# Splitting the dense weights in two GpSimd loads instead of on ScalarE and VectorE

## The chip, the core and the metric

The kernel runs on one core of a Trainium2 chip. The metric is the device time of one execution in microseconds; the median of two runs is 1895.24 us (1895.2 to 1895.29). Engines are named as in the profile: PE is TensorE, with PEld its weight loads, DVE is VectorE, ACT is ScalarE, POOL is GpSimd, SP is SyncE. SPq, ACTq and POOLq are the queues that these engines' own sequencers work off, and L233 is line 233 of the kernel before.

## The reference

One inference step of a two-layer streaming encoder, for 512 prompt tokens and 32 sample tokens of width 1024, all in float32. Layer 0 mixes tokens with an S5 state-space model and a gated unit, layer 1 with retention (4 heads). Each layer then attends to 256 memory tokens and ends in a ConvFFN of width 2816. Nearly all of the arithmetic is dense products of the 544 tokens with weight matrices:

```python
def conv_ffn(h, conv_state, w_up, conv_w, conv_b, w_down):
    u = h.astype(F32) @ w_up.astype(F32)
    a, g = jnp.split(u, 2, axis=-1)
    ext = jnp.concatenate([conv_state.astype(F32), a], axis=1)
    conv = cw[0] * ext[:, 0:l] + cw[1] * ext[:, 1:l + 1] + cw[2] * ext[:, 2:l + 2] + conv_b
    y = (jax.nn.gelu(conv) * g) @ w_down.astype(F32)
```

```python
for each layer:  x += mixer(rms(x));  x += memattn(rms(x), mem);  x += convffn(rms(x))
```

## The kernel before

Tokens stand along the free dimension (544 columns, taken as two halves of 272), channels on the 128 partitions. A product of float32 accuracy is made from operands in two parts: a first part, `hi`, rounded to the format float32r, in which TensorE multiplies, and a second part, `lo`, the rest. Of the four products of parts three are computed.

The weights lie in HBM as tiles: one contiguous chunk of 128 x 1024 numbers (512 KB) holds all that one output tile of 128 channels needs of 8 key tiles. `weights` (L209) brings a tile in: SP loads it into a buffer `wr`, ACT copies it with rounding into `wh` (L206), DVE subtracts and writes the rest to `wl` (L207). Each of the three names has three buffers, so a load into `wr` needs the subtraction of the tile three before to be over, and the rounding into `wh` needs TensorE to be through with the tile three before.

`dense_k` (L228) multiplies one key tile: 3 pairs of parts by 2 halves of the tokens, 6 matmuls. `dense` (L236) does that for all key tiles of an output tile, 48 matmuls for 8 of them. There are 240 such weight tiles outside the first stage: 8 of the S5's gated unit (`w_glu`), 16 each of the memory attention's queries and outputs (`w_q`, `w_o`), 44 each of the ConvFFN's two up projections (`w_a`, `w_g`), 48 of its down projection (`w_d`; 32 of them hold 7 key tiles), 48 of the retention's projections (`w_r`) and 16 of its output (`w_ro`).

The first stage (`phase1`) computes the S5 layer and, in its gaps, the memory's keys and values; layer 1's part of these goes through `weights` too. Then come the gated unit, attention of layer 0, ConvFFN of layer 0, retention, attention of layer 1, ConvFFN of layer 1 and the last norm. The attention also calls `weights` with buffers of its own (`into`) for the memory's keys and values.

In the ConvFFN (`ffn`, L1064 on) 8, 7 and 7 pairs of tiles of `w_a` and `w_g` are followed by 8 tiles of `w_d`. For each pair POOL has five small instructions: a memset (L1083) and a copy (L1084) into the convolution's input, two copies of its last columns to an output (L1088, L1089), and the product for the 32 sample tokens (L1096).

The order of each engine's instructions is made by the framework's scheduler, which simulates the program with costs of its own when the kernel is built. Each engine then works through its list in order; an instruction that waits holds up all behind it on that engine.

Of the kernel before, what the change touches and what calls it, by code (L numbers as in the profile page):

```python
# [9 lines left out]
F32 = mybir.dt.float32  # L10
# [3 lines left out]
OP = mybir.AluOpType  # L14
# [5 lines left out]
KT = D // P            # channel tiles  # L20
TP = 512               # prompt tokens
TS = 32                # sample tokens
# [3 lines left out]
NM = 256               # memory tokens  # L26
FF = 2816
NF = FF // P
H = 4                  # heads (memory attention and retention)
EPS = 1e-6  # L30
GN_EPS = 1e-5
G = 64                 # S5 groups
C = 16                 # channels of a group
NP = 32                # pairs of groups
L = 8                  # S5 chunk
POS = 70               # dummy, 64 prompt chunks, dummy, 4 sample chunks
SLOT = 560             # elements of a general slot
# phase 1: microseconds of TensorE's work on the memory's projections between the steps of S5
F_START, F_DISC, F_NORM, F_MAT = 0.5, 28, 2, 13
KV_US = 3.5  # L40
KV_SPLIT = (1,)          # layers whose memory projections take operands in two parts
KV_RMS, KV_ROW = 1, 4      # key tiles after which the memory's norm is worked out, and applied
# steps of S5 for an eighth of the groups (M matrices, P phases, S states, C carry, O outputs, F fill)
PROLOGUE = (("M", 0), ("P", 0), ("S", 0), ("M", 1), ("C", 0), ("F", 6))
ORDER = (("S", 1), ("C", 1), ("O", 0), ("F", 4), ("M", 2), ("F", 5))
FGROUPS = (8, 7, 7)    # ConvFFN tiles between down projections
# [6 lines left out]
def constants():  # L53
    """Arrays that depend on shapes alone."""
# [27 lines left out]
def w_tiles(w, mt=None):  # L82
    """[K, M] -> [m tile, 128 of k, K/128 * 128 of m]: one contiguous chunk for an output tile."""
    k, m = w.shape
    a = w.reshape(k // P, P, m // P, P).transpose(2, 1, 0, 3)
    return a.reshape(m // P, P, (k // P) * P)


def layout(inp):
# [10 lines left out]
    def cols(a):                      # [.., n*128] -> [128, .. * n]  # L100
        a = a.reshape(-1, a.shape[-1] // P, P)
        return a.transpose(2, 0, 1).reshape(P, -1)
# [4 lines left out]
    def pair(a):                      # [G, 64] -> [(g2, p), pair]  # L107
        return a.reshape(NP, P).T

    def both(a):                      # [G, 64] -> [(2, p), G]  # L110
        return np.concatenate([a.T, a.T], axis=0)
# [7 lines left out]
    cr, ci = f["ssm_c_re"][0], f["ssm_c_im"][0]      # [G, C, 64]  # L119
# [6 lines left out]
    rt, it = cr.transpose(2, 0, 1), ci.transpose(2, 0, 1)          # [64, G, C]  # L126
    ca = np.stack([np.concatenate([rt, it]), np.concatenate([it, rt])])   # [2, 128, G, C]
    d["ca"] = ca.reshape(2, P, KT, 8 * C).transpose(2, 1, 0, 3).reshape(KT, P, 256)

    def rows(a):                      # [1024] -> [(jj, c), G]  # L130
        return np.tile(a.reshape(G, C).T, (L, 1))
# [7 lines left out]
    # values: [layer, half of columns, quarter of k, 128, 2 k tiles * 512]  # L139
# [13 lines left out]
    d["w_r"] = w_tiles(wq)            # q 8, k 8, v 16, g 16 tiles  # L153
# [17 lines left out]
class Kernel:  # L171
# [7 lines left out]
    # ---- tiles  # L179
# [13 lines left out]
    def psum(self, name, two, one):  # L193
        """TensorE's accumulators of a part of the program: two banks each, and one each."""
        self.two, self.one = two, one
        return self.tc.tile_pool(name=name, bufs=1, space=PSUM)
# [7 lines left out]
    # ---- weights: loaded, and split into parts of 12 and 12 bits  # L204
# [4 lines left out]
    def weights(self, src, n=1024, into=None, pool=False):  # L209
        raw = self.main.tile([P, 1024], F32, tag="wr", bufs=3, name=self.name("wr"))  # L210
# [10 lines left out]
    def mm3(self, out, a, b, start, stop):  # L221
        """out (+)= a^T b for operands in two parts."""
# [20 lines left out]
    def dense_open(self, src, xs):  # L243
        """The first operands of an output tile."""
# [10 lines left out]
    def dense2(self, srcs, xs, late=1, hooks=()):  # L255
        """Two output tiles, the last operands of both behind all others; hooks go in between."""
# [15 lines left out]
    def parts(self, src):  # L272
        """src [P, T] -> its two parts, in general slots."""
# [4 lines left out]
    # ---- norms: operands are gain * x; 1 / rms comes in where a product leaves PSUM  # L278
# [29 lines left out]
    def rsqrt_of(self, m, r, tmp):  # L308
        """r = m^-1/2: a first guess from the exponent's bits, and three steps r <- r (1.5 - 0.5 m r^2)."""
# [13 lines left out]
    def resid_cols(self, ps):  # L323
        """1 / rms of the tokens, 128 of them in a column; ps [128, 5] of PSUM."""
# [12 lines left out]
    def along_row(self, ps, rc, blocks):  # L337
        """Columns rc laid along the free dimension of all partitions, in PSUM."""
# [3 lines left out]
    def resid_r(self):  # L342
        """Two hooks that give 1 / rms of the tokens along a row of all partitions, self.r."""
# [19 lines left out]
    # ---- program  # L363
    def run(self):
        nc, tc, io = self.nc, self.tc, self.io
        self.ones = self.cp.tile([P, P], F32, tag="ones", name="ones")
# [3 lines left out]
        with tc.tile_pool(name="s5", bufs=1) as sp, self.psum("psum0", 0, 8) as self.pp:  # L370
            self.sp = sp
            self.phase1(sp)
        self.xp = self.ctx.enter_context(tc.tile_pool(name="x", bufs=1))
# [18 lines left out]
    def final(self):  # L392
        """The last norm: turned to tokens by rows, scaled by 1 / rms where it leaves PSUM."""
# [30 lines left out]
    # ---- memory keys and values  # L424
    def kv_units(self):
        """The projections of both layers, in pieces that fill gaps: (microseconds of TensorE, emit)."""
# [22 lines left out]
        def rms():  # L449
            """1 / rms of the memory's tokens: along a row, and in columns."""  # L450
# [14 lines left out]
        def operand(l):  # L465
            """gain * memory"""
# [28 lines left out]
        def product(l, out, a, ca, b, cb, k):  # L495
            """out (+)= a[:, ca]^T b[:, cb], in one or in two parts."""
# [50 lines left out]
    # ---- S5  # L547
    def cmul(self, eng, o, a, b, t, eng2=None):
        """o = a b of complex pairs; t: two temporaries of the same shape. o may not alias a or b."""
# [9 lines left out]
    def phase1(self, sp):  # L559
# [43 lines left out]
        # inputs in the S5 layout: [(7 - token of chunk, channel), group, chunk]  # L603
# [4 lines left out]
        # discretisation, for columns of pairs (32) and of groups (64)  # L608
# [8 lines left out]
        def exp_acc(out, x, t):  # L617
            """exp to float32's accuracy: 2^k times a polynomial."""
# [33 lines left out]
        # powers 0..8 of a = rho (cos, sin)  # L652
# [18 lines left out]
        # b_bar = (a - 1) / lam * b, times the norm's gains  # L671
# [23 lines left out]
        # u = x / rms(x)  # L695
# [26 lines left out]
        # unit phases of a^8 to the power of the chunk, and its magnitude  # L722
# [7 lines left out]
        def unit(c):  # L730
            """c / |c|, for |c| near 1"""
# [43 lines left out]
        def matrices(e):  # L775
            """What a chunk's inputs give to the state at its end, and to its own outputs."""
# [5 lines left out]
            # a^lag b_bar, as [(g2, p), pair, lag, c]; the second holds minus the imaginary part  # L782
# [31 lines left out]
        def states(e):  # L814
            """Chunk inputs to the state, turned back by the chunk's phase, scanned, turned forth."""
# [46 lines left out]
        def carry(e):  # L862
            """What the state before a chunk gives to its tokens: Re(c a^(l+1) x)."""
# [72 lines left out]
    # ---- memory attention  # L936
    def attention(self, ap, l):
# [33 lines left out]
        def soft(rows, b0, b1, src, pr, st):  # L971
            """Softmax of scores / 16, whose queries still lack 1 / rms."""
# [30 lines left out]
        def turn(pr, pss):  # L1003
            """The weights, keys by rows."""
# [4 lines left out]
            # the sample's, from the cache  # L1009
# [53 lines left out]
    # ---- ConvFFN  # L1063
    def ffn(self, l):  # L1064
# [11 lines left out]
        for n, size in enumerate(FGROUPS):  # L1076
            ys = []
            for _ in range(size):
# [3 lines left out]
                # [2 zeros, prompt, 2 cached rows, sample]  # L1082
# [26 lines left out]
    # ---- retention  # L1109
    def retention(self, rp):  # L1110
# [26 lines left out]
        def rope(tile0):  # L1137
            """Two tiles of a projection, rotated: in float32, and in parts."""
# [32 lines left out]
        def scores(d, h):  # L1171
            d.decay = decay = st([P, TP], "decay")
            nc.sync.dma_start(out=decay, in_=io["decay"][h])
            # keys by token, with the decay to the end
# [14 lines left out]
            # the sample's scores  # L1189
# [4 lines left out]
            # scores with decay, [key, query]  # L1194
# [34 lines left out]
        def outputs(d, h):  # L1229
            """By token, normalised."""  # L1230
# [131 lines left out]
```

## Time and profile before

| | |
|---|---|
| runs | 1895.2 to 1895.29 us, median 1895.24 |
| profiled execution | span 1893.0 us; the median lies 2.2 us above it |
| PE busy | 1820.2 us, 96% |
| DVE busy | 1086.7 us, 57% |
| ACT busy | 611.6 us, 32% |
| POOL busy | 384.7 us, 20% |
| mean granted TensorE clock | 0.980 |
| DMA | 178.02 MB, mean 94 GB/s; SP's queue 27.4% of 16 engines |

Times are those of one execution. In a group's row, the number behind x is how many instructions it holds, then come busy us, mean ns of one, idle time of the engine just before them and what ended it. In a row of waits stand: who waited for whom, us in total, how often, the longest. Matmuls overlap, so their mean duration is longer than the distance between them.

### The profile page before, as it was taken

Reading aid. Unit: us, or ns where it says so; the run is one execution under the profiler, and the core shown is the slowest. Engines: PE = TensorE matmul, PEld = TensorE weight load, DVE = VectorE, ACT = ScalarE, POOL = GpSimd, SP = SyncE. Lnnn points to the kernel's source line nnn. Section 1 sums busy time; section 2 is a strip of 40 time slices with the busy share of each in tenths; the row PEclk is TensorE's granted clock in tenths of the full one; section 3 lists DMA queues with packets and bytes.
Section 4 is the critical chain, followed back from the end, with each engine's and each line's share of the span. In section 5 each row is a group of like instructions: output and inputs, shape, how many; then the busy total and the mean of one; then the engine's idle time right before and its main releaser. Section 6 shows DMA issues by size and latency. Waiting matters only on the chain.

```text
span 1893.0 us, 32752 instructions
## 1 busy us (share of the span) xinstructions
PE 1820.2 (96%) x13785; PEld 1730.6 (91%) x13785; DVE 1086.7 (57%) x1848; ACT 611.6 (32%) x901; POOL 384.7 (20%) x439
## 2 busy tenths in 40 slices
PE   7868899999999999999999999999999999999998
PEld 6457789999999999999899899998999999999998
DVE  9999856545544535555644646546655554453553
ACT  3132454433323323333223122223444332232333
POOL 7685611011211202121000100100101121120221
PEclk9888989999999999999999999999999999999998
DMA  6434344122222222232222222222411222222221
GB/s 214 132 114 124 120 133 144 68 86 79 90 90 88 78 92 90 72 109 82 76 85 94 79 79 73 90 79 86 138 68 56 87 84 88 90 84 95 90 71 67
DMA packets 65970, 178.02 MB, mean 94 GB/s; under 512 B 8928, under 2 KB 18528, under 8 KB 65824
## 3 DMA queue, kind: packets, MB, share of 16 engines
q1 hardware_dynamic: 65536, 175.79, 27.4%
q8 instruction: 108, 1.77, 0.4%
q14 instruction: 38, 0.31, 0.1%
q10 hardware_dynamic: 288, 0.15, 0.0%
HBM read 162.78 MB, written 10.77 MB: 92 GB/s over the span
## 4 chain that ended last, share of the span: by engine, by line
PE 83%; DVE 2%; issue 1%; ACT 1%; ACTq 0%; DVEq 0%
PE ps L233 74%; PE ps L224 2%; PE ps L225 2%; PE ps L226 2%; PE ps L1286 1%; DVE wl L207 0%; PE ps L1275 0%; PE ps L1248 0%; PE ps L1008 0%; PE ps L1222 0%; ACT wh L206 0%; PE bank L1022 0%; DVE xl L292 0%; PE ps L329 0%; PE ps L403 0%
## 5 line engine op out<-in xcount | busy, mean ns | idle before, releaser
L206 ACT CAST wh<-wr 128x1024 fp32r<-128x1024 f32 (+1 forms) x256 | 264.6, 1037 | 810.2 <-PE ps L233 626.8
L233 PE MATMUL ps<-xh,wh 128*128 128x272 f32 x2432 | 507.5, 290 | 5.4 <-DVE x L356 3.6
L233 PE MATMUL ps<-xl,wh 128*128 128x272 f32 x2432 | 503.6, 288 | 0.0
L233 PE MATMUL ps<-xh,wl 128*128 128x272 f32 x2432 | 502.3, 288 | 0.0
L233 PE MATMUL ps<-r,wh 128*128 128x272 f32 x2688 | 449.2, 289 | 3.0 <-ACT r L901 1.6
L233 PEld LDWEIGHTS ps<-xh,wh 128*128 128x128 f32 x2432 | 380.7, 188 | 11.1 <-ACT r L298 3.7
L233 PEld LDWEIGHTS ps<-r,wh 128*128 128x128 f32 x2688 | 380.2, 189 | 6.4 <-ACT r L206 3.0
L233 PEld LDWEIGHTS ps<-xh,wl 128*128 128x128 f32 x2432 | 382.0, 188 | 2.3 <-issue 2.3
L233 PEld LDWEIGHTS ps<-xl,wh 128*128 128x128 f32 x2432 | 383.0, 189 | 0.3
L207 DVE TENSOR_TENSOR wl<-wr,wh 128x1024 fp32r<-128x1024 f32 (+1 forms) x256 | 321.8, 1260 | 92.3 <-ACT wh L206 84.2
L233 PE MATMUL ps<-r,wl 128*128 128x272 f32 x1344 | 278.0, 288 | 0.0
L233 PEld LDWEIGHTS ps<-r,wl 128*128 128x128 f32 x1344 | 211.2, 189 | 0.0
L356 DVE TENSOR_TENSOR x<-ps,x 128x544 f32<-128x544 f32 x96 | 69.3, 724 | 234.9 <-PE ps L233 234.7
L301 POOL TENSOR_TENSOR acc<-acc,r 128x544 f32<-128x544 f32 x36 | 58.8, 1633 | 453.1 <-ACT r L298 444.6
L1088 POOL COPY nco<-r 128x2 f32<-128x2 f32 x44 | 13.9, 315 | 374.5 <-DVE r L1086 374.5
L1095 DVE TENSOR_TENSOR r<-ps,rr 128x544 f32<-128x544 f32 x44 | 31.9, 725 | 96.7 <-PE ps L233 96.7
L1085 DVE TENSOR_TENSOR r<-ps,rr 128x272 f32<-128x272 f32 x44 | 19.4, 442 | 117.4 <-PE ps L233 117.4
L1146 POOL TENSOR_TENSOR r<-r,r 128x544 f32<-128x544 f32 x8 | 10.8, 1353 | 339.9 <-ACT wh L206 326.0
L1096 POOL TENSOR_TENSOR r<-r,r 128x32 f32<-128x32 f32 x44 | 34.3, 780 | 206.2 <-ACT wh L206 186.2
L206 ACT CAST r<-r 128x544 fp32r<-128x544 f32 x84 | 52.5, 650 | 65.8 <-POOL r L1096 26.2
L1093 DVE SCALAR_TENSOR_TENSOR r<-r,conv,r 128x546 f32<-128x546 f32 x88 | 69.1, 785 | 3.5 <-ACT r L1091 1.9
L207 DVE TENSOR_TENSOR r<-r,r 128x544 fp32r<-128x544 f32 x84 | 59.3, 729 | 14.5 <-ACT r L206 14.3
(354 smaller groups left out, 2109.0 us busy)
## 6 DMA issues: line engine op xcount, KB each, us to landing
wr<-in_w_r SPq DMA_DIRECT2D x48, 512.0 KB, 3.2
wr<-in_w_a SPq DMA_DIRECT2D x44, 512.0 KB, 3.2
wr<-in_w_g SPq DMA_DIRECT2D x44, 512.0 KB, 3.2
wr<-in_w_d SPq DMA_DIRECT2D x32, 448.0 KB, 3.2
wr<-in_w_k SPq DMA_DIRECT2D x16, 512.0 KB, 4.9
wr<-in_w_v SPq DMA_DIRECT2D x16, 512.0 KB, 3.6
wr<-in_w_q SPq DMA_DIRECT2D x16, 512.0 KB, 4.0
wr<-in_w_o SPq DMA_DIRECT2D x16, 512.0 KB, 3.3
```

What stands on the lines that cost most here:

```text
L206: self.nc.scalar.copy(hi, src)
L207: (self.nc.gpsimd if pool else self.nc.vector).tensor_tensor(out=lo, in0=src, in1=hi.bitcast(F32), op=OP.subtract)
L224: mm(out, lhsT=a[0], rhs=b[0], start=start, stop=False)
L225: mm(out, lhsT=a[0], rhs=b[1], start=False, stop=False)
L226: mm(out, lhsT=a[1], rhs=b[0], start=False, stop=stop)
L233: mm(ps[:, h, :TH], lhsT=ws[wi], rhs=x[xi][:, h * TH:(h + 1) * TH], start=start and n == 0, stop=stop and n == 2)
L301: add.tensor_tensor(out=self.acc, in0=self.acc, in1=sq, op=OP.add)
L356: self.nc.vector.tensor_tensor(out=self.halves(x), in0=src, in1=self.halves(x), op=OP.add)
L1085: V.tensor_tensor(out=ext[:, 2:2 + TH], in0=pa[:, 0, :TH], in1=r[:, :TH], op=OP.mult)
L1093: V.scalar_tensor_tensor(out=cv, in0=ext[:, t:t + W], scalar=cw[:, t, f:f + 1], in1=cv, op0=OP.mult, op1=OP.add)
L1095: V.tensor_tensor(out=self.halves(gr), in0=pg[:, :, :TH], in1=self.halves(r), op=OP.mult)
L1096: PL.tensor_tensor(out=gr[:, TP:], in0=gr[:, TP:], in1=cv[:, TP + 2:W], op=OP.mult)
```

## The change

After the first stage, `weights` no longer uses `wr`, the rounding copy and the subtraction. GpSimd issues a load from HBM straight into `wh`; since `wh` is float32r and the source float32, this transfer rounds. ScalarE then writes `wh` times -1 into `wl`. GpSimd issues a second load of the same 512 KB from HBM, which adds to what is in `wl`. So `wl` becomes the weight less its first part. In the first stage (`self.plain`), and where `weights` is given buffers, the old way stays under the name `weights_plain`. The other lines of the diff drop comments and docstrings.

```diff
     def weights(self, src, n=1024, into=None, pool=False):
+
+        if into is not None or self.plain:
+            return self.weights_plain(src, n, into, pool)
+        hi = self.main.tile([P, 1024], F32R, tag="wh", bufs=3, name=self.name("wh"))
+        lo = self.main.tile([P, 1024], F32R, tag="wl", bufs=3, name=self.name("wl"))
+        hi, lo = hi[:, :n], lo[:, :n]
+        self.nc.gpsimd.dma_start(out=hi, in_=src)
+        self.nc.scalar.activation(out=lo, in_=hi.bitcast(F32), func=AF.Copy, scale=-1.0)
+        self.nc.gpsimd.dma_start(out=lo, in_=src, accum_op=OP.add)
+        return hi, lo
+
+    def weights_plain(self, src, n=1024, into=None, pool=False):
         raw = self.main.tile([P, 1024], F32, tag="wr", bufs=3, name=self.name("wr"))
         self.nc.sync.dma_start(out=raw[:, :n], in_=src)
...
     def run(self):
         nc, tc, io = self.nc, self.tc, self.io
+        self.plain = True
...
             self.phase1(sp)
+        self.plain = False
```

In the changed kernel the three new lines are L216 (first load), L217 (negation) and L218 (accumulating load).

GpSimd's order changes most. Before, in the middle of layer 0's ConvFFN, it holds the five small instructions of each pair of tiles, one pair after the other (`r` are general buffers, `nco` the output of last columns):

```order
L1083 MEMSET r_4725 128x2
L1084 COPY r_4725<-cconv 128x2
L1088 COPY nco_4461<-r_4725 128x2
L1089 COPY nco_4461<-r_4725 128x2
L1096 TENSOR_TENSOR r_4734<-r_4734,r_4733 128x32
```

The same place on GpSimd in the changed kernel, two weight tiles of `w_a` and two of `w_g` (the small instructions are the same, 14 lines further down in the file):

```order
L216 DMA wh_4975<-in_w_a 128x1024
L1110 TENSOR_TENSOR r_4833<-r_4833,r_4832 128x32
L1097 MEMSET r_4953 128x2
L1098 COPY r_4953<-cconv 128x2
L218 DMA wl_4976<-in_w_a 128x1024
L216 DMA wh_5029<-in_w_g 128x1024
L1102 COPY nco_4435<-r_4953 128x2
L1103 COPY nco_4435<-r_4953 128x2
L218 DMA wl_5030<-in_w_g 128x1024
L216 DMA wh_5104<-in_w_a 128x1024
```

The 480 loads now stand between the small instructions. In 191 of the 240 tiles, as here, a tile's accumulating load stands directly ahead of the next tile's first load; in the other 49 the next tile's first load is ahead of it.

TensorE's order has changed at the start of many tiles. Before, in the same ConvFFN, where one tile (`wh_4804`) ends and the next (`wh_4880`) begins; `xh` and `xl` are the two parts of the tokens' operands:

```order
L233 MATMUL ps_4801<-xh_4310,wl_4805 128x272 x2
L233 MATMUL ps_4877<-xh_3914,wh_4880 128x272 x2
L233 MATMUL ps_4877<-xl_3915,wh_4880 128x272 x2
L233 MATMUL ps_4877<-xh_3914,wl_4881 128x272 x2
L233 MATMUL ps_4877<-xh_3932,wh_4880 128x272 x2
```

At such a place in the changed kernel, with `wh_4846` of `w_a` and `wh_4900` of `w_g`:

```order
L245 MATMUL ps_4770<-xh_4286,wl_4772 128x272 x2
L245 MATMUL ps_4845<-xh_3896,wh_4846 128x272 x2
L245 MATMUL ps_4845<-xl_3897,wh_4846 128x272 x2
L245 MATMUL ps_4899<-xh_3896,wh_4900 128x272 x2
L245 MATMUL ps_4899<-xl_3897,wh_4900 128x272 x2
L245 MATMUL ps_4845<-xh_3896,wl_4847 128x272 x2
L245 MATMUL ps_4845<-xh_3914,wh_4846 128x272 x2
```

The first four matmuls of the next tile, which need only its first part, are moved ahead of the matmuls that need this tile's second part.

## The prediction

> **What bounds the kernel now.** I read the page's busy shares first, then the stretches before and after 300 us, then the chain that ended last in order of time, then the waits, then the way of one weight tile through its queues.
>
> ```profile
> span 1893.0 us, 32752 instructions
> PE 1820.2 (96%) x13785; PEld 1730.6 (91%) x13785; DVE 1086.7 (57%) x1848; ACT 611.6 (32%) x901; POOL 384.7 (20%) x439
> 0.00:300.00 300.00, 244.77 (x1704) 204.29 (x1705) 260.03 (x484) 104.65 (x181) 174.05 (x169) 0.90 0.44 142
> 300.00:1893.00 1593.00, 1575.38 (x12083) 1526.35 (x12081) 826.63 (x1365) 506.91 (x721) 210.67 (x271) 1.00 0.25 85
> 600.00:700.00 100.00, 100.00 (x800) 100.00 (x799) 50.06 (x69) 29.45 (x35) 18.12 (x29) 1.00 0.26 87
> ```
>
> In the rows of stretches the numbers are PE, PEld, DVE, ACT and POOL busy, then the granted clock, the DMA share and GB/s. TensorE lies idle for 300.00 - 244.77 = 55.2 us in the first 300 us, which the change leaves nearly alone (it keeps the old loads there), and for 17.6 us in the other 1593 us, at a clock of 1.00. In the ConvFFN (600 to 700) it never stops: 800 matmuls in 100 us, 0.125 us each. A weight tile of 8 key tiles is 48 matmuls, 6.0 us; one of the down projections' smaller tiles, with 7, is 42, 5.25 us.
>
> ```profile
> 393.50 35.62 PE ps L233 x281
> 446.42 392.82 PE ps L233 x3132
> 883.09 1.06 ACT wh L206
> 884.17 1.23 DVE wl L207
> 959.96 47.99 PE ps L233 x382
> 1007.98 1.05 ACT wh L206
> 1490.23 386.98 PE ps L233 x3084
> ```
>
> These are pieces of the chain (start, length, what). Both ConvFFN layers are one unbroken run of dense matmuls (L233), 393 and 387 us. One retention head lasts 1007.98 - 883.09 = 124.9 us and ends with a run of eight tiles (382 matmuls). VectorE's subtraction appears only in between heads, 1.23 us each time.
>
> ```profile
> PE ps L233 <- DVE x L356: 3.6, 1, 3.6
> PE ps L233 <- ACT wh L206: 1.8, 2, 0.9
> ACT wh L206 <- PE ps L233: 626.8, 181, 14.2
> SPq L211 <- DVE wl L207: 1377.2, 242, 29.6
> L207 DVE TENSOR_TENSOR wl<-wr,wh 128x1024 fp32r<-128x1024 f32 (+1 forms) x256 | 321.8, 1260 | 92.3 <-ACT wh L206 84.2
> ```
>
> The dense matmuls waited for weights 1.8 us in all. The other way round, the rounding on ScalarE waited 626.8 us for TensorE to let go of a buffer, and the loads on SyncE's queue 1377.2 us for the raw buffer. So the old split is ready early everywhere; the 1.26 us subtraction lies wholly beside matmuls. Nothing that leaves VectorE can be won back except a few us at the heads' starts.
>
> **The change part by part.** *Removed:* 240 subtractions, VectorE's time beside other work, worth nothing but the 1.23 us at the start of each of four heads: -5 us. The 240 issues that leave SyncE's queue free transfers that nothing waits for: 0. *Kept in size:* ScalarE's rounding copy becomes a copy times -1 of the same tile.
>
> ```profile
> L206 ACT CAST wh<-wr 128x1024 fp32r<-128x1024 f32 x224 | 234.8, 1051 | 720.5 <-PE ps L233 561.4 <-issue 106.7 <-PE bank L226 24.8
> wr<-in_w_a SPq DMA_DIRECT2D x44, 512.0 KB, 3.2
> L211 SPq DMA_DIRECT2D wr<-in_w_a x44: 327/328/328, 405.1 to 1795.0; - x44
> DMA packets 65970, 178.02 MB, mean 94 GB/s; under 512 B 8928, under 2 KB 18528, under 8 KB 65824
> q1 hardware_dynamic: 65536, 175.79, 27.4%
> L1089 POOL COPY nco<-r 128x2 f32<-128x2 f32 x44 | 44.8, 1018 | 0.0
> L1088 POOL COPY nco<-r 128x2 f32<-128x2 f32 x44 | 13.9, 315 | 374.5 <-DVE r L1086 374.5
> L1083 POOL MEMSET r<- 128x2 f32 x44 | 4.2, 96 | 0.0
> L703 POOL TENSOR_TENSOR r<-r,r 128x560 f32<-128x560 f32 x7 | 17.2, 2452 | 0.4
> ```
>
> *Moved:* what used to be a short line (load, 1.05 us on ScalarE, 1.26 us on VectorE) with loads running three raw buffers ahead becomes load, 1.05 us on ScalarE, second transfer, and both transfers are issued by GpSimd, in order. In the program's order for GpSimd the accumulating load of a tile stands ahead of the first load of the next one in 191 of 240 cases. GpSimd therefore waits at the accumulating load until the first load has landed and ScalarE has negated it; what stands behind that wait is the next tile's first load, and behind this TensorE. The raw buffer that used to uncouple tiles is gone. So the pace is the sum of one tile's steps:
>
> 1. Issue of the accumulating load on GpSimd. SyncE's issue takes 0.328 us; GpSimd's other instructions take from 0.096 to 2.452 us. Bounds 0.33 and 2.45; I take 1.0, by the row nearest to it in kind and place, a small instruction of the ConvFFN (L1089, 1018 ns).
> 2. The accumulating transfer. A plain 0.524 MB costs 27.4% x 1893.0 x 0.524 / 175.79 = 1.55 us of all 16 DMA engines. The addition reads two operands and writes one. Bounds 1.55 (no dearer than a load) and 4.65 (each of three passages priced like a load); I take twice, 3.1. It is issued first on the queue, so I take it that the next load's packets follow it; the next load's issue on GpSimd is covered by it.
> 3. The next load's own packets: 1.55.
> 4. The rest of a landing: 3.2 from issue to landing, less 0.33 and 1.55: 1.3.
> 5. The negation: 1.05.
>
> Sum 1.0 + 3.1 + 1.55 + 1.3 + 1.05 = 8.0 us a tile. Where the next load stands ahead (49 of 240 tiles, 30 of the ConvFFN's 136) a landing and a negation, 2.35 us, run beside the other tile: 2.35 x 30/136 = 0.5 less. I take 7.5 us a tile. All bounds low: 0.33 + 1.55 + 1.55 + 1.3 + 1.05 - 0.5 = 5.3; all high: 2.45 + 4.65 + 1.55 + 1.3 + 1.05 - 0.5 = 10.5.
>
> Of TensorE's side: a ConvFFN layer is 68 tiles, 52 of 48 matmuls and 16 of 42, 3168 matmuls x 0.1255 us (392.82 / 3132) = 398 us, 5.85 a tile. GpSimd's own instructions (L1083 to L1096) stand between a load and its accumulation and lie beside the landing.
>
> - ConvFFN: 136 x (7.5 - 5.85) = +224.
> - Retention: 16 tiles a head need 16 x 7.5 = 120 us of 124.9; only the run of eight is short: three tiles are ready, five come 1.5 us late, 7.5 x 4 heads = +30.
> - The gated unit of S5 (8 tiles) and the two output projections (281 matmuls, 6 tiles each in a row): (5 + 3 + 3) x 1.5 = +17. The query projections lie between other work: 0.
> - Heads' starts: -5.
>
> Together +266 on the span's 1893.0: 2159. The median of the runs, 1895.24, lies 2.2 above the span, so 2161; I say 2160.
>
> Two rules of the Trainium skill bear on step 1 and step 4. L1088 and L1089 are the same copy and take 315 and 1018 ns, and the memset ahead of them 96: something beside them stretches GpSimd's reads. The Trainium skill (SBUF — State Buffer, Who interferes with whom) says that a VectorE instruction with two inputs in SBUF holds up GpSimd instructions that read SBUF, not those that only write. By this an issue, which writes descriptors, would be nearer to 0.33; the tile would take 6.8 us and the kernel about 2045. The trace agrees so far as copies and memset go; an issue it doesn't show. The Trainium skill (DMA: Bandwidth & Descriptors, Latency and other measured facts) puts the first byte at about 1 us for loads issued by GpSimd and about 0.6 for the others: 0.4 more in step 4, 7.9 us a tile, an estimate of about 2240. No row here has a GpSimd load, so I leave both out of the sum.
>
> **The rivals.**
>
> *Hidden after all.* If the accumulating transfer costs like a load and the issue like SyncE's, the tile takes 5.3 us against 5.85 and TensorE never waits. Then only the -5 us remain: 1890. For it: the low bounds, and three buffers leave 2 x 6.0 = 12.0 us from release to use, while the steps in a row are 1.0 + 2.9 (a landing less its issue) + 1.05 + 1.0 + 2.9 + 1.55 = 10.4. Against it: it needs both low ends, and the queue's order lets no two tiles overlap. It decides at 5.85 us a tile. This is the side of not slower.
>
> *The accumulating transfer is the bound.* If its price is at or above the upper end, or casting makes the first load dear too, a tile takes 10.5 us: ConvFFN 136 x 4.65 = 632, retention 4 x (168 - 125) = 172, the other 40 tiles some 80 (420 us against the 340 that TensorE spends there), so 2780. For it: nothing in the trace shows a transfer that computes, and this is the term with the widest bounds. Against it: the engines are at 27% now and the bytes only grow threefold or so.
>
> *Freed VectorE makes the kernel faster.* VectorE is busy 57% and loses some 300 us. But all of TensorE's idle time after 300 us is 17.6 us; even the whole of it gives 1878, under 1%.
>
> *The change does not do what it says:* were the first load not rounded, the second part would be zeros; as many instructions on as many bytes, and the same time.
>
> **How the numbers follow.** The pace of about 7.5 us (6.3 to 9) has 0.66, hidden 0.12, the transfer as the bound 0.18, faster through gaps 0.02, something else 0.02. The main case's own span: at 6.3 us a tile 136 x 0.45 = 61, and some 5 for the rest: 1960; at 9 us 428 + 76 for heads (4 x (144 - 125)) + 40: 2440. The range 1940 to 2680 takes in these and the nearer half of the dear transfer, at 10.0 us a tile 564 + 140 + 60 = +764, 2660; outside lie hidden, faster, and the far end of the third, 0.18 in all. About 2% (38 us) is what a measurement of this kernel can tell from no change. Faster 0.02, within 2% 0.12, slower 0.86.
>
> **What would show it.** Right: TensorE in the ConvFFN busy about 80% instead of 100, its waits on the accumulating load's wl, evenly at every tile; GpSimd idle before L218 for ScalarE's L217, and ScalarE before L217 for the landing; a ConvFFN layer of 510 us; retention heads lengthened by under 10 us. Wrong: waits on wh instead (the first load is the dear one); TensorE waiting nowhere (hidden); DMA engines busy above 90% (third case); an issue on GpSimd of 2 us or more (step 1), or a landing well over 3.2 us with idle engines (step 4).

## The result, and the profile after

The changed kernel takes 2170.78 us (median of 2 runs, 2166.18 to 2175.38) against 1895.24 us (1895.2 to 1895.29) before: 1.1455 times as long, 95% interval 1.1397 to 1.1512. The profiled execution has a span of 2164.3 us, 271.3 more than before.

The first page and the stretches of the changed kernel, with the columns as in the prediction (TensorE's matmuls, its weight loads, VectorE, ScalarE and GpSimd busy, granted clock, DMA share, GB/s):

```profile
span 2164.3 us, 32986 instructions
PE 1913.3 (88%) x13785; PEld 1797.0 (83%) x13785; DVE 804.3 (37%) x1608; ACT 608.0 (28%) x901; POOL 629.3 (29%) x919
q0 software_dynamic: 69120, 247.49, 50.8%
300.00:2164.30 1864.30, 1674.54 (x12150) 1599.61 (x12149) 562.29 (x1138) 507.85 (x727) 448.26 (x735) 0.96 0.60 137
600.00:700.00 100.00, 87.55 (x657) 85.61 (x657) 21.21 (x36) 21.05 (x24) 23.63 (x44) 0.97 0.62 143
600.00:900.00 300.00, 260.27 (x1918) 254.79 (x1918) 70.82 (x122) 69.78 (x82) 75.28 (x150) 0.95 0.62 140
```

TensorE does the same 13785 matmuls. It lies idle for 2164.3 - 1913.3 = 251.0 us (72.8 before), and is busy for 93.1 us more: both are new. In the ConvFFN it does 657 matmuls in 100 us where it did 800. The DMA engines are far from full on the mean, 0.62.

The waits of the changed kernel (who waits, for what, us in total, times, the longest), and then what its trace tells of the accumulating load, L218:

```profile
POOL wl L218 <- ACT wl L217: 1023.8, 216, 8.7
POOL wh L216 <- PE ps L245: 301.1, 112, 24.8
ACT wl L217 <- DMA wh<-in_w_d: 196.1, 43, 9.6
PE ps L245 <- DMA wl<-in_w_d: 44.9, 22, 3.6
```

```profile
L218 POOL DMA_DIRECT2D wl<-in_w_q x16: 854/886/916, 300.8 to 1555.2; - x16
who waited for it (us, times):
  PEld ps L245: 196.5, 107
  PE ps L245: 172.2, 98
...
DMA to landing us min/median/max: 5.0/5.5/8.9
```

Before, ScalarE waited for TensorE. Now TensorE waits for the second part (98 times in a matmul, 107 times in a weight load), GpSimd waits 1023.8 us in front of the accumulating load for the negation, and ScalarE waits for landings of the first part. In the ConvFFN this reads as follows, on GpSimd (start, length, what) and for the negation on ScalarE:

```profile
701.98 0.87 POOL L218 DMA_DIRECT2D wl<-in_w_g  x1 [6.54 <-ACT wl L217]
702.53 0.87 POOL L216 DMA_DIRECT2D wh<-in_w_a  x1
...
710.43 0.89 POOL L218 DMA_DIRECT2D wl<-in_w_a  x1 [6.59 <-ACT wl L217]
711.03 0.86 POOL L216 DMA_DIRECT2D wh<-in_w_g  x1
...
719.16 0.87 POOL L218 DMA_DIRECT2D wl<-in_w_g  x1 [6.51 <-ACT wl L217]
```

```profile
709.08 1.06 ACT L217 ACTIVATE wl<-wh 128x1024 fp32r<-128x1024 f32 x1 [4.72 <-DMA wh<-in_w_a]
```

The next first load goes 0.55 us after the accumulating one; 6.55 us later the negation starts, it takes 1.06, and 0.29 later the next accumulating load goes: 8.45 us for a tile, and 8.73 for the one after it.

Where the 271.3 us lie, by the same places in both traces (in each ConvFFN the first and the last copy of the convolution's last columns to their output, L1088 for the first and L1089 for the last before, L1102 and L1103 after; and the first rounding of the keys, kth, in the first and the last retention head):

| stretch | before, us | after, us | more |
|---|---|---|---|
| start to the first ConvFFN's first copy | 448.3 | 478.2 | 29.9 |
| first ConvFFN, first to last copy | 338.6 | 420.1 | 81.5 |
| its last tiles, to the first head | 97.4 | 116.4 | 19.0 |
| first to fourth head | 374.9 | 408.6 | 33.7 |
| to the second ConvFFN's first copy | 232.9 | 249.6 | 16.7 |
| second ConvFFN, first to last copy | 338.7 | 417.0 | 78.3 |
| to the end | 62.2 | 74.4 | 12.2 |

### The profile page after: what moved, and what is told of

Read it like the earlier page. It is cut to its first block, busy times and chain, and to the rows that moved or that the text cites. A ratio compares the mean times of both kernels' runs of the same rounds, so it can differ in the third digit from the quotient of the medians.

```text
span 2164.3 us, 32986 instructions
## 1 busy us (share of the span) xinstructions
PE 1913.3 (88%) x13785; PEld 1797.0 (83%) x13785; DVE 804.3 (37%) x1608; ACT 608.0 (28%) x901; POOL 629.3 (29%) x919
## 3 DMA queue, kind: packets, MB, share of 16 engines
q0 software_dynamic: 69120, 247.49, 50.8%
## 4 chain that ended last, share of the span: by engine, by line
issue 42%; PE 24%; POOL 12%; DMA 12%; DVE 8%; ACT 1%; POOLq 0%; DVEq 0%; ACTq 0%
PE ps L245 19%; POOL wl L218 4%; POOL wh L216 3%; DMA wl<-in_w_g 2%; DMA wh<-in_w_a 2%; DMA wl<-in_w_d 1%; DMA wh<-in_w_q 1%; DMA wl<-in_w_a 1%; POOL acc L313 1%; PE ps L236 1%; PE ps L238 1%; PE ps L237 1%; DMA wl<-in_w_ro 1%; DMA wl<-in_w_o 1%; DMA wh<-in_w_d 1%
## 5 line engine op out<-in xcount | busy, mean ns | idle before, releaser
L245 PE MATMUL ps<-xh,wl 128*128 128x272 f32 x2432 | 517.9, 296 | 89.9 <-DMA wl<-in_w_a 39.2
L217 ACT ACTIVATE wl<-wh 128x1024 fp32r<-128x1024 f32 (+1 forms) x240 | 250.7, 1044 | 966.0 <-DMA wh<-in_w_d 196.1
L245 PE MATMUL ps<-r,wh 128*128 128x272 f32 x2688 | 472.9, 301 | 5.3 <-ACT r L915 2.2
L245 PEld LDWEIGHTS ps<-r,wh 128*128 128x128 f32 x2688 | 406.3, 201 | 9.0 <-ACT r L206 3.0
L245 PEld LDWEIGHTS ps<-xh,wh 128*128 128x128 f32 x2432 | 391.8, 193 | 11.7 <-issue 8.8
L245 PE MATMUL ps<-r,wl 128*128 128x272 f32 x1344 | 295.1, 304 | 82.9 <-DMA wl<-in_w_d 44.9
L245 PEld LDWEIGHTS ps<-r,wl 128*128 128x128 f32 x1344 | 222.9, 200 | 93.2 <-DMA wl<-in_w_d 51.0
L218 POOL DMA_DIRECT2D wl<-in_w_r x48 | 42.0, 874 | 229.1 <-ACT wl L217 221.8
L218 POOL DMA_DIRECT2D wl<-in_w_d x48 | 42.3, 882 | 216.0 <-ACT wl L217 205.2
L218 POOL DMA_DIRECT2D wl<-in_w_a x44 | 39.0, 886 | 225.1 <-ACT wl L217 204.1
L218 POOL DMA_DIRECT2D wl<-in_w_g x44 | 38.5, 875 | 171.0 <-ACT wl L217 162.6
```

What stands on the lines that cost most here:

```text
L217: self.nc.scalar.activation(out=lo, in_=hi.bitcast(F32), func=AF.Copy, scale=-1.0)
L218: self.nc.gpsimd.dma_start(out=lo, in_=src, accum_op=OP.add)
L245: mm(ps[:, h, :TH], lhsT=ws[wi], rhs=x[xi][:, h * TH:(h + 1) * TH], start=start and n == 0, stop=stop and n == 2)
```

## The experiments

The theory is that GpSimd's queue sets the pace, because one tile's steps stand in a row on it, and that the accumulating transfer is the dearest of them. The rivals are the number of buffers, the transfers' price as such, and TensorE being disturbed by the accumulating writes. Each kernel was timed beside runs of the kernel before on the same chip, whose median was 1894.2 to 1894.9 us.

### One half of the change at a time

**The addition left out** (the second load overwrites the negative):

```diff
-        self.nc.gpsimd.dma_start(out=lo, in_=src, accum_op=OP.add)
+        self.nc.gpsimd.dma_start(out=lo, in_=src)
```

> The changed kernel, but the second load overwrites instead of adding: the addition is left out, wl holds the rounded weight, all waits, issues and their order stay. My theory (the pace is the sum of one tile's steps in GpSimd's order): the accumulating transfer falls from 3.1 to 1.55 us, the tile from 7.2 us (50 tiles from 600.60 to 959.55 us in the changed kernel) to 5.6, under TensorE's 5.85, so 1900 to 1960 us. Rival, too few buffers (a tile takes a third of the way from a buffer's release to the end of its next use): a third of 1.55 less, 6.7 us a tile, 2050 to 2100 us. Rival, the wait for two landings alone counts and the addition costs nothing: 2170 us.

Measured: 1933.19 us, ratio 1.0202 (1.0186 to 1.0217). This is in the theory's range. GpSimd's order and the buffers are as in the changed kernel (49 first loads stand ahead in both), only the addition is gone, and with it 238 of the 276 us. The transfer is not all that got shorter: the second load's issue on GpSimd takes 0.53 us where it took 0.88, and it lands after 3.7 us where it landed after 5.5 (medians).

**Only the accumulating load** (SyncE loads the raw tile, ScalarE rounds and negates, GpSimd adds):

```diff
-        self.nc.gpsimd.dma_start(out=hi, in_=src)
+        raw = self.main.tile([P, 1024], F32, tag="wr", bufs=3, name=self.name("wr"))[:, :n]
+        self.nc.sync.dma_start(out=raw, in_=src)
+        self.nc.scalar.copy(hi, raw)
```

> Only the second half of the change: the raw weight comes by SyncE's queue into wr and ScalarE rounds it into wh as before, then negates it, and GpSimd issues only the accumulating load. My theory: no first load stands behind GpSimd's wait any more, the way of a tile from a buffer's release is 1.05 + 1.05 + 0.87 + 5.5 = 8.5 us against 11.7 to 12, so 1890 to 1915 us. Rival, the addition's transfer is by itself too dear: the same two passages of the DMA engines are there, so it stays at 2100 us or more. Rival, too few buffers: 1900 us too, since the way is 8.5 us.

**Only the rounding load** (SyncE's raw load and VectorE's subtraction stay):

```diff
+        raw = self.main.tile([P, 1024], F32, tag="wr", bufs=3, name=self.name("wr"))[:, :n]
+        self.nc.sync.dma_start(out=raw, in_=src)
         self.nc.gpsimd.dma_start(out=hi, in_=src)
-        self.nc.scalar.activation(out=lo, in_=hi.bitcast(F32), func=AF.Copy, scale=-1.0)
-        self.nc.gpsimd.dma_start(out=lo, in_=src, accum_op=OP.add)
+        self.nc.vector.tensor_tensor(out=lo, in0=raw, in1=hi.bitcast(F32), op=OP.subtract)
```

> Only the first half of the change: GpSimd issues the rounding load into wh, SyncE a second plain load into wr, VectorE subtracts as before; no negation, no accumulating load. My theory: GpSimd waits only for buffers, so 1885 to 1900 us, and DMA traffic doubles without harm. Rival, a rounding load issued by GpSimd is itself dear or late: TensorE waits for wh, 1950 us or more.

Measured: 1936.13 us (ratio 1.0213, 1.0179 to 1.0246) and 1922.37 us (1.0139, 1.0121 to 1.0157). Both forecasts missed by some 20 us; neither half alone costs what the two cost together. By the marks of the table above, the rounding half alone loses nothing between the first and the last copy of a ConvFFN (-1.0 and -1.4 us); its loss lies in the stretches around the memory attentions (12.8 us before the first ConvFFN, 17.9 before the second). Which wait costs it there was not followed up. The accumulating half loses 4.7 and 8.1 us in the ConvFFN layers, and the rest elsewhere. GpSimd's queue in the page of the kernel with the accumulating loads alone, and of that with the rounding loads alone (packets, MB, share of 16 engines):

```profile
q0 software_dynamic: 34560, 123.75, 38.3%
```

```profile
q0 software_dynamic: 34560, 123.75, 20.1%
```

That is the price of each: 38.3% of 1934.0 us over 240 tiles is 3.09 us of all 16 engines for an accumulating load, and 20.1% of 1924.5 us is 1.61 us for a rounding one (means over all tiles, of which 32 hold 448 KB and not 512). The bytes counted are the same.

### Order and buffers

**The next tile's first load ahead of the accumulating load.** In the changed kernel it stands ahead at 49 of 240 tiles; here at 239. A list of the coming tiles gives the next source:

```diff
+        nxt = self.first()
...
+            with self.tc.issue_after(nxt[1].ins):
+                self.nc.gpsimd.dma_start(out=lo, in_=src, accum_op=OP.add)
```

> The changed kernel with GpSimd's order written out: each tile's first load is issued ahead of the accumulating load of the tile before it, at all tiles instead of 49 of 240; buffers still three. My theory: a landing and a negation now run beside the other tile; what is left is that the load ahead must wait for the release of a buffer, then 0.55 + 0.87 us of issues and 5.5 us of landing, 7.3 us to the next tile's use, and two tiles take 7.3 + 5.85, 6.6 us a tile: 2000 to 2050 us. Rival, too few buffers from the start: no gain or a loss, 2170 us or more. Rival, the DMA engines' price of the addition: 2170 us.

Measured: 2186.46 us, ratio 1.1532 (1.1493 to 1.157). The theory's forecast failed: the order alone brings nothing, and the time is in the rivals' range. The wait had moved, as the kernel's waits and its GpSimd rows show:

```profile
POOL wh L232 <- PE ps L292: 1351.1, 227, 30.0
```

```profile
704.70 0.55 POOL L232 DMA_DIRECT2D wh<-in_w_a  x1 [4.43 <-PE ps L292]
705.23 0.92 POOL L222 DMA_DIRECT2D wl<-in_w_g  x1
...
714.21 0.60 POOL L232 DMA_DIRECT2D wh<-in_w_g  x1 [7.63 <-issue]
714.81 0.92 POOL L222 DMA_DIRECT2D wl<-in_w_a  x1
...
719.22 0.55 POOL L232 DMA_DIRECT2D wh<-in_w_a  x1 [2.73 <-PE ps L292]
```

Now the first load waits for TensorE to let go of a buffer, and the accumulating load of the tile in hand stands behind that wait: two tiles take 719.22 - 704.70 = 14.52 us. The landing of an accumulating load, whose packets now follow a first load's, had a median of 7.9 us. So from the release to the landing pass 0.5 + 7.9 = 8.4 us, and with three buffers only one tile of matmuls, 5.85 us, lies beside them.

**A fourth buffer for first parts,** first alone, and then with that lookahead. Two general slots fewer make the room:

```diff
-        t = self.main.tile([P, SLOT], dt, tag="r", bufs=28, name=self.name("r"))
+        t = self.main.tile([P, SLOT], dt, tag="r", bufs=26, name=self.name("r"))
...
-        hi = self.main.tile([P, 1024], F32R, tag="wh", bufs=3, name=self.name("wh"))
+        hi = self.main.tile([P, 1024], F32R, tag="wh", bufs=4, name=self.name("wh"))
...
```

> The changed kernel with four buffers for first parts instead of three (two general slots fewer make the room); GpSimd's order of instructions is the same. Theory (queue order): load, landing, negation and accumulating load of one tile still follow one another on GpSimd's queue, some 8 us a tile whatever the number of buffers, so 2150 to 2180 us, as the changed kernel. Rival (buffers): the next load waits for TensorE to let go of a buffer, so a fourth one gives a tile's time of slack and the time falls clearly, to 2050 us or less.

> The kernel with the next tile's first load issued ahead of the accumulating load, and four buffers for first parts. Theory after that kernel with three buffers took 2186 us: there TensorE's release of tile k-2 lets load k+1 go, the accumulating load of k stands behind it and lands some 8.5 us later, and only one tile of 5.85 us covers this: (8.5 + 5.85) / 2 = 7.2 us a tile, as measured. With four buffers two tiles cover it, 11.7 us, so the ConvFFN is hidden again: 1900 to 1950 us. Rival (price of the engines or the addition's latency is what bounds): 2100 us or more, with or without a fourth buffer.

Measured: 1918.75 us (ratio 1.0132, 1.0117 to 1.0147) and 1922.66 us (1.0148, 1.0133 to 1.0163). The second time is as forecast. The first expectation was wrong, and in a premise too: GpSimd's order did not stay. With a fourth buffer the program itself puts the next first load ahead at 239 of 240 tiles, so both kernels have the same order there. From the kernel with the fourth buffer alone, a stretch of the ConvFFN and GpSimd's rows:

```profile
600.00:700.00 100.00, 99.67 (x796) 99.45 (x794) 34.20 (x59) 31.88 (x38) 34.89 (x69) 1.00 0.80 168
```

```profile
715.45 0.56 POOL L216 DMA_DIRECT2D wh<-in_w_g  x1 [2.66 <-PE ps L245]
716.90 0.87 POOL L218 DMA_DIRECT2D wl<-in_w_a  x1 [0.89 <-ACT wl L217]
720.70 0.56 POOL L216 DMA_DIRECT2D wh<-in_w_a  x1 [2.93 <-PE ps L245]
722.03 0.87 POOL L218 DMA_DIRECT2D wl<-in_w_g  x1 [0.77 <-ACT wl L217]
```

Here too a first load waits for a release, but now two tiles, 11.7 us, lie beside the way from it to the landing. TensorE is busy for 99.67 of 100 us and the DMA engines for 0.80. The loads are the same and no cheaper: GpSimd's queue takes 60.0% x 1917.6 / 240 = 4.79 us of all 16 engines for a tile, against 50.8% x 2164.3 / 240 = 4.58 in the changed kernel. So the price alone is not what bounded the changed kernel.

**Four buffers, but every first load behind the accumulating load before it,** which tells the order from the buffers:

```diff
-        self.nc.gpsimd.dma_start(out=hi, in_=src)
...
+            with self.tc.issue_after(self.last):
+                self.nc.gpsimd.dma_start(out=hi, in_=src)
...
-        self.nc.gpsimd.dma_start(out=lo, in_=src, accum_op=OP.add)
+        self.last = self.nc.gpsimd.dma_start(out=lo, in_=src, accum_op=OP.add).ins
```

> Four buffers for first parts, as in the kernel that took 1918.75 us, but every first load is placed behind the accumulating load of the tile before it on GpSimd's queue (there it stands ahead of it at 239 of 240 tiles, in the changed kernel at 49). Theory (order): the steps of one tile follow one another whatever the number of buffers, 8.1 to 8.7 us a tile as in the stretches of the changed kernel where no load was ahead; 136 x (8.4 - 5.85) = 347 us in the ConvFFN and some 100 elsewhere: 2250 to 2350 us. Rival (the fourth buffer did it, whatever the order): 1950 us or less.

Measured: 2343.66 us, ratio 1.2369 (1.2346 to 1.2391), as the theory of the order forecast. GpSimd's rows in this kernel's ConvFFN:

```profile
701.50 0.89 POOL L222 DMA_DIRECT2D wl<-in_w_g  x1 [3.37 <-ACT wl L221]
702.10 0.86 POOL L220 DMA_DIRECT2D wh<-in_w_a  x1
...
709.70 0.87 POOL L222 DMA_DIRECT2D wl<-in_w_a  x1 [2.42 <-ACT wl L221]
...
717.86 0.90 POOL L222 DMA_DIRECT2D wl<-in_w_g  x1 [3.21 <-ACT wl L221]
```

A tile takes 8.20 and 8.16 us, far above TensorE's 5.85: with this order a fourth buffer does not hide the chain. The cases together, in us:

| first loads ahead | three buffers | four buffers |
|---|---|---|
| none of 240 | not tried | 2343.66 |
| 49 of 240 | 2170.78 (the change) | not tried |
| 239 of 240 | 2186.46 | 1918.75 and 1922.66 |

With the first load behind, the steps of a tile are a chain on GpSimd. With it ahead and three buffers, TensorE's release of a buffer is in the chain. Only with it ahead and four buffers is nothing in the chain that TensorE's work doesn't cover.

### What freeing VectorE is worth, and what is left

**No subtraction, nothing in its place** (the first part stands in for the second, whose rest this kernel leaves out):

```diff
+        if into is None and not self.plain:
+            self.nc.scalar.copy(hi, raw[:, :n])
+            return hi, hi
```

> The kernel before, without the subtraction after the first stage: the first part stands in for the second too, so the second parts of the weights are left out of what is computed. This is the most that freeing VectorE could give with nothing put in its place. Theory: the subtraction lies beside matmuls, 1885 to 1893 us. Rival (VectorE's load costs time elsewhere): 1870 us or less.

Measured: 1884.71 us, ratio 0.9951 (0.9934 to 0.9967). The whole gain to be had is 9.5 us, half a per cent.

**The old split up to the first ConvFFN,** with four buffers, and **26 general slots in the kernel before:**

```diff
-        self.plain = False
         self.xp = self.ctx.enter_context(tc.tile_pool(name="x", bufs=1))
...
+            self.plain = False
             self.ffn(0)
```

> Four buffers for first parts and the changed loads from the first ConvFFN on; the gated unit of S5 and the first memory attention (24 tiles) keep the old split. With the changed loads there too the first ConvFFN began 15.6 us later than in the kernel before, which is most of the 24 us that were left. Theory (the rest of the loss comes from these first tiles, whose loads stand behind the S5 stage's work on GpSimd): 1900 to 1907 us. Rival (it comes from anywhere a stage begins, by a cost of the loads as such): 1912 us or more.

```diff
-        t = self.main.tile([P, SLOT], dt, tag="r", bufs=28, name=self.name("r"))
+        t = self.main.tile([P, SLOT], dt, tag="r", bufs=26, name=self.name("r"))
```

> The kernel before with 26 general slots instead of 28, and nothing else: the room that the fourth buffer of the other kernels took. In two of them (the one with four buffers, and the one whose first 24 tiles keep the old split) TensorE was some 9 to 11 us less busy between 100 and 260 us, in the S5 stage, than in the kernel before. Theory (the missing slots cost this, not the loads): 1902 to 1907 us, so that of the 24 us left with four buffers only some 14 belong to the changed loads. Rival (26 slots are enough): 1893 to 1897 us.

Measured: 1914.11 us (ratio 1.0108, 1.0093 to 1.0123) and 1893.67 us (0.9996, 0.9986 to 1.0005). Both theories failed: each against the kernel before on its own chip, 19.5 of the 24.6 us are left when the 24 tiles keep the old split, and the missing slots cost nothing. The 24 us that four buffers leave stay open in part. By the marks of the table above, that kernel reaches the first ConvFFN's first copy 15.6 us later than the kernel before (463.9 against 448.3), loses 2.6 and 2.4 us in the two ConvFFN layers and next to nothing in retention. With the old split there it still comes 9.8 us late (458.1), most of it between 100 and 260 us, in the S5 stage, where no load was changed. The order of instructions did change there: in both kernels the orders of VectorE, GpSimd, ScalarE and TensorE are those of the kernel before up to some 107 us, and differ from there on, while with 26 slots alone they stay the same at least up to 230 us. That this order costs the time fits, but was not tried by itself.

### Does TensorE's clock need the writes?

In the changed kernel TensorE's granted clock falls in places. The matmuls that end a pause of 2.48 us, and then windows of 2 us around it:

```profile
707.45 0.52 PE L245 MATMUL ps<-xh,wl 128*128 128x272 f32 x2 [2.48 <-DMA wl<-in_w_g]
```

```profile
705.00:707.00 2.00, 0.00 (x0) 0.00 (x0) 0.88 (x4) 0.00 (x0) 0.00 (x0) 1.00 1.00 223
707.00:709.00 2.00, 1.55 (x12) 1.55 (x13) 0.00 (x0) 0.00 (x0) 0.00 (x0) 0.97 0.57 205
709.00:711.00 2.00, 2.00 (x10) 2.00 (x10) 0.10 (x1) 1.79 (x2) 0.57 (x1) 0.50 0.00 0
711.00:713.00 2.00, 2.00 (x13) 2.00 (x13) 1.47 (x2) 0.46 (x1) 1.65 (x4) 0.67 0.38 45
```

Two kernels make such pauses with no load on GpSimd and no addition: the kernel before with a single raw buffer after the first stage, and the rounding copy done twice, or four times. Both also have 26 general slots, which by themselves cost nothing (above). The diff is that of the copy done twice.

```diff
-        raw = self.main.tile([P, 1024], F32, tag="wr", bufs=3, name=self.name("wr"))
+        one = into is None and not self.plain
+        raw = self.main.tile([P, 1024], F32, tag="w1" if one else "wr", bufs=1 if one else 3, name=self.name("wr"))
...
+        if one:
+            self.nc.scalar.copy(hi, raw[:, :n])
         self.split(raw[:, :n], hi, lo, pool)
```

> The kernel before, slowed by other means: one raw buffer instead of three after the first stage, and the rounding copy done twice, so that load (3.2 us), two copies (2.1), subtraction (1.26) and handovers (0.3) follow one another, 6.9 us a tile against TensorE's 5.85. No load is issued by GpSimd and none adds. Both theories put the time at 2030 to 2080 us, by the pace; they differ in TensorE's busy time. Pauses alone lower the granted clock and stretch matmuls: clock under 0.98, TensorE busy 1860 us or more (1820 in the kernel before, 1913 in the changed one). Rival (the accumulating writes disturb TensorE): clock 0.99 or more, TensorE busy 1835 us or less.

> The kernel before with one raw buffer after the first stage and the rounding copy done four times: load, 4 x 1.05 us, subtraction and handovers follow one another, some 9.4 us a tile (7.28 us were measured with two copies). No load is issued by GpSimd, none adds. TensorE pauses some 3 us a tile. Theory (a pause of TensorE of over about 2 us is by itself followed by some 3.4 us at half the clock): the granted clock in the ConvFFN falls to 0.95 or less, as in the changed kernel (0.95), with stretches at 0.5 after most of the long pauses; the time goes by the pace, 2330 to 2400 us. Rival (it takes the accumulating writes): the clock stays at 0.99 or 1.00 in the ConvFFN.

Measured: 2072.21 us (ratio 1.0938, 1.0921 to 1.0954) and 2540.13 us (1.3416, 1.3394 to 1.3439; the pace was slower than forecast). With two copies the test was too weak: of the pauses of the ConvFFN between 600 and 800 us the longest was 1.94 us, only one was followed by half the clock (of 1.78 us), and the clock of the whole run was 0.978 against 0.980. TensorE was still busy 1886.8 us, but much of the rise is not the clock: between 600 and 800 us its 1306 matmuls count as busy for 177.87 us at a clock of 0.99, where 0.1255 us each would be 163.9. So busy time alone doesn't tell the theories apart. With four copies, the matmuls that end a pause of 3.69 us, a ConvFFN stretch, and the windows after the pause:

```profile
644.02 1.27 PE L236 MATMUL ps<-r,wh 128*128 128x272 f32 x4 [3.69 <-ACT wh L206]
```

```profile
600.00:700.00 100.00, 79.07 (x528) 74.15 (x527) 26.97 (x34) 49.78 (x50) 2.39 (x10) 0.91 0.17 57
644.00:646.00 2.00, 1.98 (x7) 1.68 (x8) 1.86 (x2) 0.00 (x0) 0.00 (x0) 0.50 0.00 0
646.00:648.00 2.00, 2.00 (x11) 2.00 (x11) 0.00 (x0) 0.00 (x0) 0.00 (x0) 0.50 0.73 262
650.00:652.00 2.00, 2.00 (x18) 2.00 (x17) 0.00 (x0) 1.94 (x3) 0.00 (x0) 1.00 0.00 0
```

The clock is 0.91 with the DMA engines at 0.17 and no accumulating write: pauses suffice. Nor do the writes alone do it: with four buffers and no pauses, in the stretch shown above, the same accumulating loads go on at a clock of 1.00, and 796 matmuls take 99.67 us, 0.125 each as before the change.

## Why the prediction was right, point by point

The time was right, 2160 us against 2170.78, and so was the mechanism: GpSimd's order strings one tile's steps in a row. But some terms were off in opposite directions, so that the closeness of the time is in part luck, and one rival was turned down for an incomplete reason.

- **The removed subtraction** was put at -5 us, at the heads' starts. Alone it is worth 9.5 us, but not there: by the marks of the table above, the kernel without it gains 0.3 us between the first and the fourth head, 5.9 before the first ConvFFN and 4.1 between the fourth head and the second ConvFFN.
- **Step 1, the issue on GpSimd,** 1.0 us (0.33 to 2.45): 0.87 us. The next issue starts 0.55 us after it, so in the chain it counts for that. The lower value that the prediction drew from the Trainium skill (SBUF — State Buffer, Who interferes with whom), nearer to 0.33, is not what the rows have: the first loads' issues took 0.53 to 0.91, the accumulating ones 0.85 to 0.92.
- **Step 2, the accumulating transfer,** 3.1 us (1.55 to 4.65): 3.09. Two passages' worth was right. **Step 3,** 1.55: 1.61.
- **Steps 2 to 4 together,** 3.1 + 1.55 + 1.3 = 5.95: 6.55 us from the first load's issue to the negation. The Trainium skill (DMA: Bandwidth & Descriptors, Latency and other measured facts) puts loads issued by GpSimd about 0.4 us later than others; the 0.6 that the step was short lies on that side, but no row separates the first byte. **Step 5,** 1.05: 1.06.
- **The sum for a tile in a row,** 8.0: 8.45 and 8.73 in the rows of the changed kernel, 8.2 in those of the kernel with every first load behind.
- **Where a load stands ahead** the prediction took off 2.35 us, 0.5 on the mean. This was the term most in error. The pace of the first ConvFFN, from the first accumulating load of a stretch at 502.2 to the 41st at 793.7, is 291.5 / 40 = 7.29 us (7.5 forecast): some 1.2 to 1.4 are taken off on the mean. In the two ConvFFN layers an accumulating load whose first load stood ahead goes a median of 1.7 us after the one before it, and the others 8.4. The 8.0 was too low and the 0.5 taken off too little; the two errors cancel, which is why 7.5 came so near to 7.29. One such place, in GpSimd's rows:

```profile
681.34 0.90 POOL L218 DMA_DIRECT2D wl<-in_w_a  x1 [3.38 <-ACT wl L217]
...
683.24 0.88 POOL L218 DMA_DIRECT2D wl<-in_w_g  x1 [0.49 <-ACT wl L217]
684.47 0.55 POOL L216 DMA_DIRECT2D wh<-in_w_a  x1 [0.35 <-PE ps L245]
...
693.32 0.88 POOL L218 DMA_DIRECT2D wl<-in_w_a  x1 [7.08 <-issue]
```

Two tiles take 11.98 us here instead of 2 x 8.45: with both first loads landed, the second tile goes 1.90 us after the first. So 4.9 us are saved, over half a chain, where the prediction had 2.35.

- **The stages.** ConvFFN +224: 191 at most (81.5 + 19.0 + 78.3 + 12.2 of the table, whose second and fourth hold a little else). Retention +30: 33.7 for three of the four heads; "under 10 us" a head became 11.2. The other projections +17: most of 29.9 + 16.7, from the stages around the memory attentions, where the prediction had taken the query projections at nothing. What was too much in the ConvFFN was too little there.
- **What would show it.** Right: 1918 matmuls in 300 us of the ConvFFN against 2389 before, 80%; GpSimd in front of L218, ScalarE in front of L217; DMA engines under 90%; issue under 2 us. Not as written: TensorE's busy time says 87%, not 80, since it ran part of the time at a lower clock; and the waits on the second part come at some 100 of 240 tiles, in matmul or weight load, and not at every one: some tiles follow their predecessor closely, as above.
- **Hidden after all** was tied to both low prices, and against it stood that "the queue's order lets no two tiles overlap". The second was the one that mattered: with the order turned and a fourth buffer loads of 4.79 us of engines for a tile are hidden. Where the prediction says "the pace is the sum of one tile's steps", it should have said: as long as the order and three buffers hold.
- **The transfer as the bound** needed 10.5 us a tile. Both loads use 50.8% x 2164.3 / 240 = 4.58 us of the engines, under TensorE's 5.85. **Faster by a free VectorE:** its most is the 0.5% above. Whether the first load rounds as it says changes no time, and no run here bears on it.

## What to carry to other kernels

When a step on an engine is replaced by a second transfer on an in-order queue, work out two loops before any price: what stands ahead of the next load on the queue, and from which release to which landing the buffers must reach. Here four combinations of order and buffers gave 1919 to 2344 us with loads of the same kind, and neither the order nor the fourth buffer alone brought the time below the changed kernel's. And when the engine to be relieved is waited for nowhere, drop its work alone first: that run put the whole possible gain at half a per cent.

## What the runs showed of the hardware

- **An accumulating load costs twice a plain one in engine time,** 3.09 us against 1.55 for a tile of 512 KB into SBUF, though its queue counts the same bytes; a rounding load costs about as much as a plain one, 1.61. The accumulating load's issue on GpSimd takes longer too, 0.88 us against 0.53 without the addition, and its landing 5.5 against 3.7. Leaving out the addition took the share of GpSimd's queue from 4.58 to 40.7% x 1931.6 / 240 = 3.28 us a tile.
- **Short pauses halve TensorE's clock.** In the changed kernel between 600 and 800 us all five pauses of 2.2 us or more were followed, at once or up to 1.4 us later, by 3.4 us at a granted clock of 0.50; of the ten shorter ones a single one was, of 1.75 us, while one of 1.90 was not. In the kernel with four copies a pause of 1.75 us was followed by such a stretch, and one of 2.10 was not; so there is no sharp length. In the changed kernel's 200 us the slow stretches start at 606.5, 671.3, 708.9, 726.0, 766.9 and 787.4 us, which lie 19, 11, 5, 12 and 6 times 3.41 us apart: where a pause falls on this grid seems to matter beside its length, which was not tried. The Trainium skill (TensorE: Matmul & The Clock Gate, What's actually happening) tells of a window of about 3.4 us that runs on by itself, and a clock that is full or half. The 0.50, the length of the stretches and the grid of their starts agree with it; that it takes an idle window of that length does not, since pauses of half of it were enough here.
- **What that is worth here** is not settled to the last. In the 300 us of the ConvFFN TensorE lies idle for 39.7 us and runs 1918 matmuls in 260.27 us, which at the 0.1255 us of before would be 240.7: 19.6 us of slower matmuls beside 39.7 of waiting. Over the whole run a mean clock of 0.949 in 2164.3 us, against 0.980 in 1893.0, is an estimated 72 us of clock lost more than before, the greater part of the 93.1 us for which TensorE is busy longer. Where GpSimd's chain sets the pace, slower matmuls only fill a pause; where a first load waits for a release, as at 112 tiles of the changed kernel and 227 of that with the lookahead, they lengthen the chain.
